# A two-layer hybrid mixer step on one core: TensorE's order fixed by a tracing weaver, with projections kept in DRAM

## The chip, the core and the metric

The kernel runs on one core of a Trainium2 chip as one launch. The metric is the device time of an execution in microseconds; the median of three runs of the kernel before is 1660.7 us (1656.93 to 1663.94). The profile is of a single execution, with its own time.

## The reference

One inference step of a bidirectional diffusion backbone with two layers, in float32, over 1280 tokens (256 of a prompt, which scan themselves from zero states, and 1024 latent tokens, which scan from cached states), model width 1024. Cut to what matters, per layer:

```
mod = silu(c) @ w_ada + b_ada                       # shift, scale, gate; for prompt and latent
h   = rmsnorm(x, g) * (1 + scale) + shift
proj = h @ w_in                                     # aq ak av ao az ag | bq bk bv bz | cq ck cv cz clr
A (4 heads x 128): stabilised chunkwise mLSTM, gates ag; times sigmoid(ao)
B (4 heads x 64):  retention, 2-D rotary on latent queries and keys
C (4 heads x 32/64): gated linear attention, decay from clr @ gla_w2
each: one scan forward + one backward, summed; y = head_rms(.) * headnorm_g * silu(az|bz|cz)
x   = x + gate * (y @ w_out)
```

At the end come a final RMS norm and the context's last states of both layers as outputs.

## The kernel before

The 1280 tokens are ten chunks of 128. The normalised input `h` stays in SBUF in two parts (a rounded high part and the rest), and every projection is three matmuls per 128 rows of `w_in` (`TERMS`, L467), accumulated in one of two PSUM banks `pj`. There are two forms. `mm_fm` (L469) has features on the partitions, in token blocks of 256, 512 and 512: 24 matmuls per block, 72 for 128 features; it serves queries, keys and the gates of `gate_z` (L1229). `mm_tm` (L488) has tokens on the partitions, 256 features for a pair of chunks: 48 matmuls per pair, 240 for all ten chunks; it serves values (`proj_v`, L516), output gates (`proj_o`, L1111) and `out_proj` (L1330). `gates` (L554) projects 304 columns per chunk (C's values and the small gate inputs). Weights come through two `raw` buffers and are split by ScalarE and VectorE (L433).

The mixers work in float32, in small steps that go through TensorE, ScalarE, VectorE and GpSimd in turn, in six PSUM banks `mx`. `mlstm_rows` (L580) makes the mLSTM's rows of weights and writes them to DRAM, `decays` (L660) C's cumulated decays. `group_c` (L743), `group_b` (L1017) and `head_a` (L1121, once for each of four heads) have the same two phases: a *key phase* over ten chunks (transpose the keys, scale them, multiply by the values, update the states) and an *output phase* over five pairs of chunks (scores, masking by decay weights, products, head norm, transposes, store). Their inputs and states live in twelve tiles of an arena `f5` (L128), which `proj_feat` (L508), `proj_v` and `proj_o` take as well. Every result goes to a DRAM tile `yd`, except the heads a2 and a3, whose results stay in the arena. `gate_z` reads it, multiplies by the gated projection and writes it back; `out_proj` loads all of it into the place of `h`.

The order of a layer is a hand-written string, which `layer` (L1247) goes through step by step:

```
"g v0 cq ck m d k1 C q0 k0 o0 a0 q1 z7 bg a1 z6 br bt bk0 bg bk1 bq0 bg bg bg bq1 be bv z1 B bg bg k2 "
"v1 bg bg q2 bg z0 bg bg k3 o1 bg a2 q3 a3 bg z5 z2 bg z4 z3 bg bg bg",          # layer 0
```

(`m` is `mlstm_rows`, `d` is `decays`, `bg` a piece of the background work that computes modulations on VectorE, 16 units in layer 0.) The string sets only the order of tracing and so of buffers. The order of each engine's instructions comes from the framework's scheduler, which lists instructions by simulated readiness and priority. Projections' matmuls are traced at a very low priority (`late`, L165), score matmuls at a high one and chained (`run`, L152), so that the scheduler puts projections wherever mixers leave room. DMAs are issued by SyncE, in the order of its queue.

## Time and profile before

| | |
|---|---|
| median of three runs | 1660.7 us |
| profiled execution, its own time | 1658.01 us |
| its span | 1656.2 us |
| mean granted TensorE clock | 0.980 |
| TensorE busy (matmul) | 1562.5 us, 94% |
| VectorE / ScalarE / GpSimd busy | 983.5 / 607.8 / 128.4 us |
| instructions | 28729 |
| DMA moved | 167.51 MB, mean 101 GB/s |

The span runs from the first to the last instruction. A matmul counts as busy from its issue to its modelled end, so neighbouring matmuls overlap, and the pace of a dense run is read from starts, not from the mean duration. The granted clock is 1.00 at 2.4 GHz; a mean of 0.98 over a stage says that TensorE ran part of it at 1.2 GHz. A float32 matmul of a mixer has two records, a transpose one.

### The profile page before, as it was taken

Reading aid. Unit: us, or ns where it says so; the run is one execution under the profiler, and the core shown is the slowest. Engines: PE = TensorE matmul, PEld = TensorE weight load, DVE = VectorE, ACT = ScalarE, POOL = GpSimd, SP = SyncE. Lnnn points to the kernel's source line nnn. Section 1 sums busy time; section 2 is a strip of 40 time slices with the busy share of each in tenths; the row PEclk is TensorE's granted clock in tenths of the full one; section 3 lists DMA queues with packets and bytes.
Section 4 is the critical chain, followed back from the end, with each engine's and each line's share of the span. In section 5 each row is a group of like instructions: output and inputs, shape, how many; then the busy total and the mean of one; then the engine's idle time right before and its main releaser. Section 6 shows DMA issues by size and latency. Waiting matters only on the chain.

```text
span 1656.2 us, 28729 instructions
## 1 busy us (share of the span) xinstructions
PE 1562.5 (94%) x11014; PEld 1423.2 (86%) x11014; DVE 983.5 (59%) x2510; ACT 607.8 (37%) x1587; POOL 128.4 (8%) x215
## 2 busy tenths in 40 slices
PE   6899889999999998999999889899999999999997
PEld 2898779887889897889999878899888989988997
DVE  3477765486778855863454676556336643465545
ACT  5546324333112324342365362244411223434323
POOL 1200010000001001000021000100000100000001
PEclk9999999999999999999999998999999999999999
DMA  9213143433424534561141031424233142336203
GB/s 326 71 41 83 49 115 92 140 118 104 123 62 129 163 101 118 191 183 38 36 161 39 18 87 29 122 77 115 59 88 100 34 136 80 111 109 189 64 14 130
DMA packets 169344, 167.51 MB, mean 101 GB/s; under 512 B 19101, under 2 KB 144957, under 8 KB 169197
## 3 DMA queue, kind: packets, MB, share of 16 engines
q1 hardware_dynamic: 169024, 165.53, 33.4%
q8 instruction: 88, 1.44, 0.4%
q14 instruction: 60, 0.48, 0.1%
q10 hardware_dynamic: 172, 0.05, 0.0%
HBM read 129.49 MB, written 27.85 MB: 95 GB/s over the span
## 4 chain that ended last, share of the span: by engine, by line
PE 66%; DMA 13%; DVE 12%; ACT 4%; issue 2%; SPq 1%; POOL 0%; DVEq 0%; POOLq 0%; ACTq 0%
PE pj L477 25%; PE pj L496 23%; DMA f<-in_w_ada_dram 3%; PE pj L567 3%; DMA rw<-rrow 3%; DMA f<-f 3%; PE mx L1203 2%; PE mx L1152 2%; DVE f L333 2%; DMA wk<-yd 2%; PE mx L1205 2%; PE mx L1194 1%; DVE f L535 1%; DVE lo L439 1%; PE mx L417 1%
## 5 line engine op out<-in xcount | busy, mean ns | idle before, releaser
L477 PE MATMUL pj<-hA,hi 128*128 128x512 f32 (+1 forms) x1408 | 373.3, 347 | 2.3 <-ACT f L504 2.3
L496 PE MATMUL pj<-hi,hA 128*128 128x256 f32 x1728 | 343.6, 286 | 5.7 <-ACT f L1118 2.2
L496 PEld LDWEIGHTS pj<-hi,hA 128*128 128x128 f32 x1728 | 276.3, 190 | 9.5 <-ACT f L1118 2.8
L477 PEld LDWEIGHTS pj<-hA,hi 128*128 128x128 f32 x1408 | 243.4, 191 | 31.1 <-ACT f L504 2.7
L496 PE MATMUL pj<-hi,hB 128*128 128x256 f32 x1152 | 240.4, 287 | 10.3 <-ACT f L504 6.3
L477 PE MATMUL pj<-hB,hi 128*128 128x512 f32 x704 | 237.2, 406 | 4.9 <-ACT f L504 2.5
L496 PE MATMUL pj<-lo,hA 128*128 128x256 f32 x864 | 241.0, 285 | 0.0
L477 PE MATMUL pj<-hA,lo 128*128 128x256 f32 (+1 forms) x704 | 240.7, 346 | 0.0
L496 PEld LDWEIGHTS pj<-hi,hB 128*128 128x128 f32 x1152 | 188.8, 190 | 12.7 <-ACT f L504 7.1
L439 DVE TENSOR_TENSOR lo<-raw,hi 128x256 fp32r<-128x256 f32 (+2 forms) x193 | 118.4, 625 | 114.3 <-ACT hi L438 107.6
L496 PEld LDWEIGHTS pj<-lo,hA 128*128 128x128 f32 x864 | 161.5, 189 | 0.3 <-issue 0.2
L496 PE MATMUL pj<-lo,hB 128*128 128x256 f32 x576 | 161.6, 285 | 0.0
L477 PEld LDWEIGHTS pj<-hB,hi 128*128 128x128 f32 x704 | 132.4, 192 | 33.7 <-ACT f L504 3.2
L438 ACT CAST hi<-raw 128x256 fp32r<-128x256 f32 (+2 forms) x193 | 106.5, 564 | 133.8 <-PE pj L477 98.0
L477 PEld LDWEIGHTS pj<-hA,lo 128*128 128x128 f32 x704 | 134.3, 191 | 14.8 <-issue 0.5
L477 PE MATMUL pj<-hB,lo 128*128 128x512 f32 x352 | 142.2, 404 | 0.0
L333 DVE SCALAR_TENSOR_TENSOR f<-f,sc 128x256 f32<-128x256 f32 x224 | 97.2, 479 | 23.2 <-DMA f<-in_w_ada_dram 23.1
L496 PEld LDWEIGHTS pj<-lo,hB 128*128 128x128 f32 x576 | 108.2, 190 | 0.0
L374 ACT ACTIVATE rw<-f 128x256 bf16<-128x256 f32 (+1 forms) x90 | 43.3, 482 | 112.3 <-DVE f L1374 106.3
L504 ACT COPY f<-pj 128x256 f32<-128x256 f32 (+2 forms) x142 | 48.5, 390 | 87.7 <-PE pj L496 48.0
L477 PEld LDWEIGHTS pj<-hB,lo 128*128 128x128 f32 x352 | 67.4, 192 | 14.7
L1371 DVE TENSOR_TENSOR wk<-pj,f 128x512 f32<-128x512 f32 (+1 forms) x45 | 28.3, 630 | 83.3 <-PE pj L496 82.6
(276 smaller groups left out, 2486.8 us busy)
## 6 DMA issues: line engine op xcount, KB each, us to landing
raw<-in_w_in_dram SPq DMA_DIRECT2D x64, 512.0 KB
f<-in_w_ada_dram SPq DMA_DIRECT2D x32, 384.0 KB
wk<-yd SPq DMA_DIRECT2D x48, 256.0 KB
rw<-rrow SPq DMA_DIRECT2D x40, 256.0 KB
rw<-wrow SPq DMA_DIRECT2D x40, 256.0 KB
f<-in_w_ada_dram SPq DMA_DIRECT2D x16, 512.0 KB
f<-in_x_sample_dram SPq DMA_DIRECT2D x16, 512.0 KB
raw<-in_w_out_dram SPq DMA_DIRECT2D x32, 256.0 KB
```

The source lines that it names most:

```text
L333: dve.scalar_tensor_tensor(acc[v], w, scv[:, k, v:v + 1], acc[v], ALU.mult, ALU.add)
L374: act.activation(rw().bitcast(BF16)[:, 0:x.shape[1]], x, AF.Square, accum_out=out)
L438: act.copy(hi[:, e], raw[:, e])
L439: dve.tensor_tensor(lo[:, e], raw[:, e], hi[:, e].bitcast(F32), ALU.subtract)
L477: pe.matmul(ps[:, :n], lhsT=w[wi][:, k, :], rhs=hblk(xi, k, b), start=(i == 0), stop=(i == 23))
L496: end = pe.matmul(pv[:, u, :], lhsT=hchunk(xi, k, c), rhs=w[e // 4][wi][:, e % 4, :], start=(i == 0), stop=(i == 23))
L504: act.copy(out, ps)
L567: pe.matmul(ps, lhsT=hchunk(xi, k, c), rhs=w[k // 3][wi][:, k % 3, :], start=(i == 0), stop=(i == 23))
L1152: pe.matmul(U[d], lhsT=ks[:, d * P:(d + 1) * P], rhs=v[:, c, :], start=True, stop=True)
L1203: pe.matmul(po[:, d, :], lhsT=r4[:, d, e, :], rhs=v[:, c, :], start=True, stop=not inter)
L1205: pe.matmul(po[:, d, :], lhsT=wb[:, d, e * P:(e + 1) * P], rhs=S[d][:, c, :], start=False, stop=True)
L1371: dve.tensor_tensor(t, pv, row.unsqueeze(1).to_broadcast([P, len(cs), 256]), ALU.mult)
```

## The change

Tracing is turned into cooperative threads. Each mixer, the chain of projections of the layers, the modulations, the norms and the gate multiplications become Python generators, which yield `wait(gap, cond, tiles needed)`. A weaver holds a clock that counts the traced matmuls' estimated cost, always continues the first thread (mixers before projections) whose gap has passed, whose condition holds and whose tiles are free, and chains every TensorE instruction to the one before it. So TensorE's order is the order of tracing. The other engines' instructions are still placed by the scheduler, but those of a mixer's visit not ahead of the last TensorE instruction traced before the visit.

```diff
+        def visit(self, th):
...
+            for ins in nc.cur_bb.bb.instructions[n:]:
+                if ins.engine == mybir.EngineType.PE:
+                    if self.tail is not None:
+                        edge(ins, self.tail, mybir.DependencyReason.DATA)
+                    self.tail = ins
+                    clock[0] += cost(ins)
+                elif th.mixer and tail is not None:
+                    edge(ins, tail, mybir.DependencyReason.SCHED_ONLY)
+            th.ready = clock[0] + gap
+
+        def run(self):
+            while self.threads:
+                best, kept = None, 0
+                for th in self.threads:
+                    n = th.need.get(f5, 0)
+                    t = None if n and len(f5.free) < kept + n else th.time()
+                    kept += n if th.cond is None or th.cond() else 0
+                    if t is not None and (best is None or t < best[0]):
+                        best = t, th
+                        if t <= clock[0]:
+                            break
...
+                clock[0] = max(clock[0], best[0])
+                self.visit(best[1])
```

`mm_fm` and `mm_tm` yield after pieces of 6 matmuls of 512 columns or 12 of 256; `late`, `run`, `not_before` and their priorities go. Both layers have one order, in which a `+` says that the projection's result is stored to DRAM slots `sp` and fetched by its mixer:

```diff
-    "g cq v0 ck m q0 d C k0 k1 o0 z6 br a0 q1 a1 bv bq0 bk1 z7 bt bk0 bq1 be z1 v1 q2 B z0 k2 k3 o1 a2 q3 "
-    "a3 z5 z2 z4 z3",
+    "g cq+ ck+ C k0+ v0+ q0+ o0+ a0 k1+ q1+ a1 bk0+ bk1+ bq0+ bq1+ bv+ B v1+ k2+ q2+ k3+ q3+ o1+ a2 a3 z",
```

```diff
+    def put(out, x, f):
+        if out[0].tensor.name == sp.tensor.name:
+            stage = wk()
+            f([v3(stage[:, x * i:x * i + x], o.shape[-1]) if len(o.shape) == 3 else stage[:, x * i:x * i + x]
+               for i, o in enumerate(out)])
+            for i, o in enumerate(out):
+                act.dma_start(o, v3(stage[:, x * i:x * i + x], o.shape[-1]) if len(o.shape) == 3
+                              else stage[:, x * i:x * i + x])
+        else:
+            f(out)
...
+    def fetched(x):
+        t, name = x
...
+            t = f5()
+            sync.dma_start(t, src)
```

A mixer's gaps stand in its generator. `decays` comes first, then `mlstm_rows` (gaps 9, 7, 8, 6, 2.5, 6) and `group_c` beside each other. The start and the loops of `group_c` and `head_a`, and the demand of `group_b`:

```diff
+    def group_c(l, e, finished):
...
+        yield wait(0, cond=lambda: "B" in e and "ck" in e, f=4, rw=1)
...
         for p in range(2):
+            yield wait(6.0, rw=1)
...
+        yield wait(7.0, mx=2, sm=2, sta=2)
...
+        for i in range(NCH + 1):
...
+            yield wait(2.5, mx=1, sm=1, sta=int(i < 2))
...
+        yield wait(0, cond=lambda: not inside, mx=4, rw=2)
+        inside.append(1)
+        tiles, yn = scores(0), None
+        for c0 in range(0, NCH + 2, 2):
+            yield wait(5.0, mx=2, rw=1, wk=1, ti=1)
...
+                yield wait(2.0, mx=4, rw=2)
+                tiles = scores(c0 + 2)
+        inside.clear()
...
+    def head_a(l, hd, e, finished):
+
+        yield wait(0, cond=lambda: "rows" in e, f=4, sta=2)
...
+        yield wait(6.0, mx=2, sm=2)
...
+            yield wait(2.2, mx=1, sm=1)
...
+        yield wait(0, cond=lambda: not inside, f=1, rw=4, sm=2)
...
+        yield wait(4.0)
+        weights(0, ahead[0])
+        yield wait(3.0, mx=1, rw=2, sm=1)
...
+        for c0 in range(0, NCH + 2, 2):
+            yield wait(5.0, mx=3, wk=1, ti=3)
...
+    def group_b(l, e, finished, general):
+        yield wait(0, f=9, sta=3, sm=1)
```

`group_b` then has four gaps of 7 (one per rotated tile), one of 8, ten of 2.5 in its keys, and 5.0 and 2.0 per output round. A mixer that is over lets `fillers` run its `gate_z`, behind the layer's projections in rank; `out_proj` waits until all of `gate_z` and, in layer 0, the modulations are done. The modulations become one thread of 16 units. Further edits: every head's result goes through `yd`, those of a2 and a3 too (`gate_z` and `out_proj` read them there); weight loads and their splits are traced with a priority 400 instructions ahead; the head norm of B and C works on two chunks at once; C's keys are scaled in three blocks; keys of the next chunk are transposed ahead of the products of the last; `mlstm_rows` needs three arena tiles instead of five; `rw` has 7 buffers instead of 8, `sm` 5 instead of 4, `ti` 8 instead of 4.

## Rows read from the trace of the kernel before

**Rows 1.** part 1 of the page: busy us, share of the span, instructions

```profile
PE 1562.5 (94%) x11014; PEld 1423.2 (86%) x11014; DVE 983.5 (59%) x2510; ACT 607.8 (37%) x1587; POOL 128.4 (8%) x215
```

**Rows 2.** busy time by stage: width, each engine (x instructions), PEclk, DMA share, GB/s

```profile
81.50:742.70 661.20, 626.60 (x4301) 564.65 (x4299) 462.78 (x1223) 232.59 (x601) 49.30 (x76) 0.98 0.39 113
...
898.00:1532.00 634.00, 609.50 (x4187) 552.30 (x4188) 352.74 (x920) 223.56 (x580) 44.91 (x66) 0.98 0.32 91
...
1532.00:1656.20 124.20, 111.25 (x910) 109.79 (x908) 64.18 (x167) 38.85 (x119) 5.43 (x10) 0.96 0.20 69
```

**Rows 3.** the same view of finer stages

```profile
180.00:260.00 80.00, 70.90 (x607) 64.36 (x608) 54.03 (x142) 21.97 (x57) 11.38 (x13) 0.96 0.29 80
...
898.00:990.00 92.00, 82.85 (x506) 72.99 (x506) 62.28 (x106) 43.97 (x66) 2.76 (x4) 0.96 0.25 64
...
990.00:1060.00 70.00, 61.41 (x480) 54.22 (x481) 46.05 (x112) 19.55 (x48) 7.21 (x7) 0.88 0.22 61
...
1060.00:1240.00 180.00, 178.27 (x1240) 164.58 (x1239) 87.34 (x254) 67.77 (x211) 13.69 (x26) 1.00 0.32 89
```

**Rows 4.** who waited for whom, TensorE: total us, times, longest us

```profile
PE mx L654 <- DVE sm L652: 8.8, 6, 2.2
PE pj L496 <- ACT f L504: 7.6, 7, 4.8
...
PE mx L811 <- DVE f L771: 3.7, 2, 3.2
```

**Rows 5.** TensorE's timeline at the layers' borders: start us, us, line, tiles, count

```profile
86.69 0.30 PE L567 MATMUL pj<-lo,hB 128*128 128x304 f32 x1
...
734.35 0.39 PE L477 MATMUL pj<-hB,lo 128*128 128x512 f32 x1
...
897.63 0.30 PE L567 MATMUL pj<-lo,hB 128*128 128x304 f32 x1
...
992.07 0.87 PE L811 MATMUL mx<-cst,f 128*128 128x128 f32 x6 [3.19 <-DVE f L771]
...
1525.42 0.39 PE L477 MATMUL pj<-hB,lo 128*128 128x512 f32 x1
```

**Rows 6.** the chain that ended last, two dense runs of projections: start us, us

```profile
1189.02 52.94 PE pj L477 x274
...
1535.54 82.53 PE pj L496 x676
```

**Rows 7.** TensorE's timeline, four float32 matmuls of a mixer

```profile
1301.51 0.66 PE L1028 MATMUL mx<-f,sm 128*128 128x128 f32 x4
...
1301.93 0.36 PE L496 MATMUL pj<-hi,hA 128*128 128x256 f32 x1
```

**Rows 8.** VectorE's timeline, first and last full-width operation of L580's rows

```profile
902.67 0.82 DVE L587 COPY f<-f 36x1280 f32<-36x1280 f32 x1
...
931.95 1.47 DVE L624 TENSOR_TENSOR f<-f,ti 36x1280 f32<-36x1280 f32 x1
```

**Rows 9.** ScalarE: one group by line (busy, mean ns, idle before); one DMA issue

```profile
L504 ACT COPY f<-pj 128x256 f32<-128x256 f32 (+2 forms) x142 | 48.5, 390 | 87.7 <-PE pj L496 48.0 <-PE pj L477 19.7 <-PE pj L567 15.5
...
1.17 0.47 ACTq L195 DMA_DIRECT2D wk<-in_headnorm_g_dram  x1
```

**Rows 10.** DMA queue (packets, MB, share); SyncE's longest waits (total, times, longest)

```profile
q1 hardware_dynamic: 169024, 165.53, 33.4%
...
SPq L445 <- DVE lo L439: 168.1, 28, 32.4
```

**Rows 11.** the chain at the end of layer 1: start us, us

```profile
1508.19 2.05 DMA yd<-wk
1510.25 3.21 DMA wk<-yd
```

More of the change, by code (lines that the diff above doesn't have):

```diff
@@ L100, in __init__, with take, give @@
         def __init__(self, name, n, cols, space=sb, dt=F32):
[L101 to L102 removed]
+            self.free = [space.tile([P, cols], dt, tag=f"{name}{i}", name=f"{name}{i}") for i in range(n)]
+            self.n, self.at = n, {}
         def __call__(self):
[L105 to L106 removed]
+            t = self.take()
+            self.give(t)
+            return t
+        def take(self):
+            return self.free.pop(0)
+        def give(self, *tiles):
+            for t in tiles:
+                self.free.append(t)
+                self.at[id(t)] = clock[0] + HELD
     class Arena:
@@ new lines, in wait, with cost @@
+    def wait(gap=0.0, cond=None, **need):
+        return gap, cond, {pools[k]: n for k, n in need.items()}
+    def cost(ins):
+        out, lhs = ins.outs[0].bass_ap, ins.ins[0].bass_ap
+        n = 1
+        for a in out.shape[1:]:
+            n *= a
+        if out.shape[0] < 2 or lhs.shape[0] < 64 and n > 64:
+            return 0.06
+        if ins.is_transpose:
+            return 0.11
+        if lhs.dtype == F32R:
+            return 0.007 + 0.441 * n / 1000
+        return 2 * max(0.109, 0.84 * n / 1000) * (0.5 if lhs.shape[0] < P else 1)
@@ L430, in norm_h, with norm_thread @@
             f5.give(*xn)
+    def norm_thread(l, b, xn, done):
+        yield wait(5.0, mx=1, rw=1)
+        for k in range(KT):
+            norm_h(l, b, xn, [k])
+            if k < KT - 1:
+                yield wait(0.9, mx=1, rw=1)
+        done.add(b)
     def split(raw, parts=1, cols=1024):
@@ L603, in mlstm_rows @@
         dve.tensor_tensor(r, F, m, ALU.subtract)
-        mp, rl_, al = (ti()[0:R, 0:NCH] for _ in range(3))
+        yield wait(8.0)
+        small = [ti.take() for _ in range(3)]
+        mp, rl_, al = (t[0:R, 0:NCH] for t in small)
         mc = v3(m, P)
@@ new lines, in group_b @@
+        fin = ring[2]
+        last = None
+        yield wait(8.0, mx=2, sm=2)
+        for i in range(len(order) + 1):
+            if i < len(order):
+                bank = mx.take()
+                now = bank, keys(1, order[i], bank[:, 0:256])
+            if i > 0:
+                c, (bank, ks) = order[i - 1], last
+                U = products(ks, c, bank[:, 256:512])
+                if c == 0:
+                    update(fin, sbv(0), U, 1)
+                    state_out(fin, 1)
+                else:
+                    update(sbv(c - 1), sbv(c) if c != 1 else None, U, 1)
+                mx.give(bank)
+            last = now
+            yield wait(2.5, mx=1, sm=1)
@@ L1430, in program, with modulations, layers @@
                 late_setup()
-        for l in range(2):
-            out_proj(l, layer(l, general, w))
+        anchor[0] = None if general else adas[-1].ins
+        normed, prepared = set(), set()
+        def modulations():
+            yield wait(40.0)
+            yield from background()
+            prepared.add(0)
+        def layers():
+            yield wait()
+            yield from layer(0, general, w, lambda c: True, lambda: general or prepared)
+            yield from out_proj(0, normed)
+            yield from layer(1, general, w, lambda c: (c + 2) // 4 in normed, lambda: True)
+            yield from out_proj(1, normed)
+        weave.add(layers(), 2)
+        if not general:
+            weave.add(modulations(), 1)
+        weave.run()
         pn = mx()
```

1070 lines of the change are left out of this document (630 added, 440 removed), and 2 rows, old and new, of the table ORDER.

## The prediction

> **What bounds the kernel now.** I read the busy shares first: TensorE is busy 94% of a span of 1656.2 us [rows 1], so only its order, its waits and its clock can move the time. By stage, the two stretches of projections and mixers hold 661 and 634 us, with 34.6 and 24.5 us in which TensorE has nothing, while VectorE is at 70% and 56% [rows 2]. These holes lie close together. Finer stages show 9.1 us in 180 to 260 and 9.2 and 8.6 us in 898 to 990 and 990 to 1060, where the granted clock falls to 0.96 and 0.88; the 180 us behind, with two heads in work, lose 1.7 us at a clock of 1.00 [rows 3]. So mixers woven densely into projections can be nearly free, and the holes are stages without enough projections to put between them. TensorE's waits agree: behind the start none is longer than 5 us, and they are on small mixer steps and on evacuations into arena tiles [rows 4]. An evacuation there waits until one of twelve tiles is free.
>
> The layers' borders give the two lengths that the change acts on [rows 5]: from the last gate matmul to the last matmul of `gate_z`, 87.0 to 734.7 in layer 0 (647.7 us) and 897.9 to 1525.8 in layer 1 (627.9 us). Start, output projections and end (380 us together) keep their order and tiles; I take them over.
>
> **Work in a layer.** 274 projection matmuls over features took 52.94 us and 676 over tokens 82.53 us [rows 6]: 0.193 and 0.122 each. `proj_feat` and `gate_z` run 22 times with 72 matmuls (13.9 us each, 306 us); the five token projections 240 each (29.3 us, 147 us). Layer 1's stage holds 4187 matmuls; without these 2784 and some 50 of the next stage, 1350 are the mixers'. Four of theirs took 0.42 us [rows 7], so at most 142 us, and less where row tiles run side by side; I estimate 110 to 142. TensorE's work is thus 563 to 595 us per layer, 33 to 85 us under what the layers take now. Spilled tiles make projections independent of the arena, so they can fill every hole while they last. That is the gain.
>
> **The mixers' chain.** The new order has a length of its own. One mixer at a time may be in its output phase (`inside`), group B needs nine of the twelve arena tiles, and each visit comes a traced gap after the one before. A gap ends at a piece's border; pieces are 6 matmuls of 512 or 12 of 256 columns, 1.4 us, so a gap costs 0.7 more on average. Own matmuls of a visit are priced at 0.21 (two records). Counted from the end of the gates:
> - C waits for cq and ck (28 + 2.5), then gaps 6, 6, 7 (21), 11 key visits of 2.5 + 0.7 + 0.7 (43) and five output rounds of 12 with a last visit (64): 158.
> - a0 and a1, keys done meanwhile: prelude 9, six gaps of 5.7, matmuls 12, so 55 each: 268.
> - B is traced behind ten feature and three token projections (227) and the mixers' matmuls so far (50): 277. Four rotations of 7.7 and 8.7 (39), ten key visits of 3.9 (39), outputs 80: 435.
> - a2 cannot load before B returns its tiles: 48 for loads and keys, 55 for outputs: 538. a3 outputs 51, with less to put between: 589. The last `gate_z` piece set, 14: **603**.
> This is more than the work, so the chain sets the layer's length: for its last part the projections have run out and TensorE waits for a2 and a3. The half pieces weigh most: some 95 gaps are on the chain, so without them it is 536, under the work; with whole pieces 670.
>
> **New waits.** TensorE's order is fixed, so a visit that comes too early holds every projection piece behind it, and the evacuations behind those.
> - Start of a layer. C's first key transposes stand about 51 us behind the gates (30 + 21). Now they start 94 us behind them (992.1 against 897.9) [rows 5], after the mLSTM rows, the decays and C's preparation. The rows' stretch on VectorE took 31 us (902.7 to 933.4) [rows 8]; they no longer have to come first, but share VectorE. 94 - 31 = 63, 12 late; I take 14. Bounds: 0, as VectorE was idle for 30 of these 92 us [rows 3], and 43, if nothing overlaps.
> - Layer 0 also carries the sixteen modulation units; its VectorE is busier by 110 us [rows 2]. I add 5; bounds 0 and 20.
> - Output visits. Not priced above 0; bounds 0 and 20 per layer, one late microsecond for each of some twenty visits in the filled part; in the dense stage of two heads TensorE lost 1.7 us in 180 [rows 3], the nearest row, hence 0.
> - Stores. Each layer evacuates 42 feature blocks through `wk` with one DMA from ScalarE and 25 token pairs with two: 92 issues of 0.47 [rows 9], 43 us of ScalarE, which is busy 233 of 661 us [rows 2]. An evacuation of 0.39 [rows 9] plus one or two issues is under the 2.8 us of the shortest block, with two banks: 0. Bounds 0 and 43, all uncovered.
> - Loads. SyncE gets some 60 more DMAs per layer; it stood up to 32.4 us before a weight load whose buffer was in use [rows 10], and a fetch behind such a wait is late by what is left of it. Fetches are traced a phase ahead: 0, bounds 0 and 32 once a layer.
> - End of a layer. y2 and y3 now go through DRAM; a store and a load took 2.05 and 3.21 [rows 11]. `out_proj` takes these blocks last: 2, bounds 0 and 5.3.
> - Merged head norms, C's keys scaled in three blocks and one row tile fewer change VectorE and GpSimd by a few us each way, beside work that already covers them: 0.
>
> **One rule weighed.** The queue moved 165.5 MB in 33.4% of the engines' span [rows 10]. Spilled slots add 24 x 0.66 MB of stores and some 19 MB of loads per layer, about 70 MB: by the row, 48%.
> The Trainium skill (DMA: Bandwidth & Descriptors, "Issuing engines are not separate DMA queues") says that DMAs from ScalarE and SyncE share the same 16 engines, so the second queue buys issue time only. By that rule the stores slow the loads: if landing times grew with the share, the layer's end would cost 3 where I took 2. No run here shows both queues loaded.
>
> **The sum.** Layer 0: 603 + 14 + 5 + 2 = 624 instead of 647.7, -23.7. Layer 1: 603 + 14 + 2 = 619 instead of 627.9, -8.9. Together -32.6: a span of 1623.6. The profiled execution took 1658.0 with its span of 1656.2, so 1625.4; the median of the three runs is 2.7 above it. On that scale: **1628 us**, 2% faster.
>
> **Rivals.**
> - *The work sets the end* (0.16). If gaps cost little more than their traced length, the chain is under the work and projections last to the end: layers of about 580, -67.7 and -47.9, so 1656 - 116 + 4.5 = 1545. For it: the dense 180 us [rows 3]. Against it: a2 and a3 both stand behind B.
> - *Waits move, none go* (0.12). What a hole cost is paid at the fixed visits: 1661, at most some us either way. For it: most holes are at layer starts, where VectorE's chain of rows, decays and preparation is the same.
> - *VectorE is late for the fixed order* (0.30). At the start of a layer C's keys are 28 late instead of 14, and some twenty output visits 1 us each: 603 + 28 + 20 + 2 = 653, in layer 0 658. That is +10.3 and +25.1, so 1696. Stalls of 32 us per layer decide: 603 + 32 + 2 is the present mean of 638. For it: TensorE has no other instruction to take while it stands, and VectorE, at 68% in 898 to 990 [rows 3], is what C's first keys wait for already, up to 3.2 us [rows 4]. Against it: its idle 30 us in that stretch.
> - That values stay in the arena after all is excluded: every name in the new order has the sign for the spill, and every mixer fetches.
>
> **How the numbers follow.** The forecast case has 0.42 and reaches from 1605 to 1650: layers 12 shorter to 11 longer than in the sum. About 0.5% (8 us) is what a measurement of this kernel can tell from no change. Faster: 0.42 + 0.16 = 0.58; same 0.12; slower 0.30. For 8 in 10 the range takes in most of the first rival and of the slow one, and the half pieces' bounds: 1555 to 1700.
>
> **What would show it.** TensorE's idle time in 180 to 260 and 990 to 1060 should fall under 3 us per stage, at a clock near 1.00. A wait of 10 us or more at C's first transposes in each layer would show the start's price, named as a wait for VectorE; none would take 28 us off. Sparse TensorE between the last `gate_z` of B and that of a3, with granted clock at 1.2 GHz there in part, would show the chain; a dense end there would prove the first rival. More than ten output visits that wait a microsecond or more for VectorE would prove the slow one, and a wait of an evacuation for a store would show that the stores are not hidden. The prediction is wrong if either layer, gates' end to last `gate_z`, takes under 590 or over 650 us.

## The result and the profile after

The changed kernel takes 1787.5 us (median of 4 runs, 1782.6 to 1789.5) against 1662.3 in the same comparison (1656.9 to 1665.2): ratio 1.0753, 95% interval 1.0715 to 1.0791. It is 125 us slower. The forecast was 1628, and the result lies above its range, which ended at 1700. The profiled execution took 1789.2 with a span of 1787.4, at a mean granted clock of 0.950 (0.980 before).

Part 1 of the page after, and the busy time by stage, cut at the gates' end and the last `gate_z` of each layer (width, engines, granted clock, DMA share, GB/s):

```profile
PE 1598.8 (89%) x11014; PEld 1457.6 (82%) x11014; DVE 987.6 (55%) x2458; ACT 607.5 (34%) x1555; POOL 113.0 (6%) x193
```
```profile
89.50:781.80 692.30, 619.84 (x4197) 561.12 (x4196) 450.63 (x1174) 216.89 (x554) 42.30 (x66) 0.96 0.49 151
781.80:975.80 194.00, 173.76 (x1296) 168.13 (x1294) 80.81 (x159) 80.48 (x212) 11.55 (x20) 0.93 0.27 84
975.80:1637.70 661.90, 609.30 (x4138) 552.21 (x4137) 345.80 (x880) 214.07 (x550) 40.78 (x62) 0.97 0.44 134
1637.70:1787.40 149.70, 127.17 (x963) 122.88 (x961) 75.56 (x185) 47.63 (x137) 5.44 (x10) 0.90 0.30 93
```

These answer to [rows 1, 2]. TensorE's matmuls fill 89% of the span instead of 94%, while VectorE and ScalarE have within 5 us the work that they had, and GpSimd 15 us less: TensorE stood more. It was also slower where it worked: the same 11014 matmuls fill 36 us more (1598.8 against 1562.5). In the traces TensorE is busy at the lower level of the clock, 1.2 GHz, for 121 us here and for 53 before. Half of that difference, 34 us, is an estimate of what the clock alone cost. The other 95 of the 131 us by which the spans differ are time without a matmul. By the borders of [rows 5], layer 0 takes 692 us instead of 647.7, layer 1 662 instead of 627.9, the stretch between them 194 instead of 163.3, the stretch behind layer 1 150 instead of 130.8: 44 + 34 + 31 + 19 = 128 of those 131. So two things went wrong, inside the layers and at their ends, and the forecast had the second at 2 us a layer.

What TensorE waited for (total us, times, longest us), in answer to [rows 4], and the timeline of C's second key transposes in each layer, in answer to the line of L811 in [rows 5] (the first had stood alone since 146.68 and 1029.57):

```profile
PE mx L1554 <- DVE rw L1576: 28.2, 9, 6.6
PE mx L998 <- DVE f L953: 25.2, 2, 12.9
PE mx L1554 <- DVE rw L1507: 21.4, 20, 2.7
PE pj L579 <- ACT hA L1686: 19.2, 13, 5.5
PE mx L1247 <- DVE sm L1249: 13.3, 8, 3.1
PE mx L1254 <- DVE sta L1266: 10.8, 8, 1.7
PE pj L579 <- ACT wk L588: 9.7, 2, 7.3
...
PE mx L429 <- DVE f L419: 3.3, 1, 3.3
```
```profile
159.23 0.45 PE L998 MATMUL mx<-cst,f 128*128 128x128 f32 x1 [12.28 <-DVE f L953]
...
1042.75 0.47 PE L998 MATMUL mx<-cst,f 128*128 128x128 f32 x1 [12.90 <-DVE f L953]
```

Before, the largest of these groups was 8.8 us. Now there are five of over 10 us inside the mixers (L1554 twice, L998, L1247, L1254; 99 us together) and one at `out_proj` (L579 waiting for the casts of y, 19.2). C's keys stand for 12.3 and 12.9 us, close to the 14 that the forecast gave them. The 20 waits at L1554 for L1507 are one pattern inside the visits of `head_a`. One of these visits, with the other engines' rows between:

```profile
333.11 0.61 PE L1506 MATMUL mx<-f,f 128*128 128x128 f32 x4
...
333.84 0.68 DVE L1507 TENSOR_TENSOR rw<-rw,mx 128x512 f32<-128x512 f32 x1
...
334.57 0.44 PE L1554 MATMUL mx<-cst,rw 128*128 128x128 f32 x2 [0.85 <-DVE rw L1507]
```

The four score matmuls (L1506) go to one half of a PSUM bank, VectorE multiplies them into a tile (L1507, from 333.84 for 0.68), and the transposes of the round before (L1554), which read no result of that multiplication, go to the bank's other half. They start at 334.57, 0.05 after VectorE is done. In a fixed order nothing else may go in between.

The Trainium skill (PSUM — Partial Sum Buffer, "PSUM bank collisions raise a hardware error") gives the rule to guard accesses to PSUM with semaphores by bank and quadrant of partitions, or simply by bank, not by address. The trace agrees with a guard by bank: the transposes touch no address that VectorE reads, and yet they wait until the read's end.

In the kernel before, none of these groups shares a bank with work that does not depend on it. There the scores have a bank of their own, the transposes go into the bank of their own round's products, and B's keys take one bank per chunk. So the change did two things here: it put these groups into halves of one bank, which the description above does not list, and it fixed their order.

### The profile page after: what moved, and what is told of

It is laid out like the page before. It is cut to its first block, busy times and chain, and to the rows that moved or that the text cites. A ratio compares the mean times of both kernels' runs of the same rounds, so it can differ in the third digit from the quotient of the medians.

```text
span 1787.4 us, 29167 instructions
## 1 busy us (share of the span) xinstructions
PE 1598.8 (89%) x11014; PEld 1457.6 (82%) x11014; DVE 987.6 (55%) x2458; ACT 607.5 (34%) x1555; POOL 113.0 (6%) x193
## 5 line engine op out<-in xcount | busy, mean ns | idle before, releaser
L566 PE MATMUL pj<-hA,hi 128*128 128x256 f32 (+1 forms) x1408 | 366.0, 351 | 7.6 <-DVE wk L1597 7.6
L579 PE MATMUL pj<-hi,hA 128*128 128x256 f32 x1728 | 340.6, 297 | 24.4 <-ACT hA L1686 19.2
L579 PEld LDWEIGHTS pj<-hi,hA 128*128 128x128 f32 x1728 | 285.5, 202 | 33.4 <-ACT hA L1686 23.4
L566 PEld LDWEIGHTS pj<-hA,hi 128*128 128x128 f32 x1408 | 243.4, 196 | 34.3 <-DVE wk L1597 8.4
L579 PE MATMUL pj<-lo,hA 128*128 128x256 f32 x864 | 252.2, 292 | 0.0
L566 PE MATMUL pj<-hA,lo 128*128 128x512 f32 (+1 forms) x704 | 241.8, 343 | 0.0
L579 PE MATMUL pj<-hi,hB 128*128 128x256 f32 x1152 | 215.8, 288 | 9.7 <-ACT wk L588 9.7
L566 PE MATMUL pj<-hB,hi 128*128 128x512 f32 x704 | 223.8, 399 | 0.0
L579 PEld LDWEIGHTS pj<-hi,hB 128*128 128x128 f32 x1152 | 182.4, 195 | 10.6 <-ACT wk L588 10.1
L579 PEld LDWEIGHTS pj<-lo,hA 128*128 128x128 f32 x864 | 173.9, 201 | 0.0
L579 PE MATMUL pj<-lo,hB 128*128 128x256 f32 x576 | 164.6, 286 | 0.0
L566 PEld LDWEIGHTS pj<-hA,lo 128*128 128x128 f32 x704 | 137.2, 195 | 15.5
L566 PEld LDWEIGHTS pj<-hB,hi 128*128 128x128 f32 x704 | 128.6, 189 | 24.9
L566 PE MATMUL pj<-hB,lo 128*128 128x512 f32 x352 | 138.2, 393 | 0.0
L579 PEld LDWEIGHTS pj<-lo,hB 128*128 128x128 f32 x576 | 112.1, 195 | 0.0
L419 DVE SCALAR_TENSOR_TENSOR f<-f,sc 128x256 f32<-128x256 f32 x224 | 96.2, 479 | 16.3 <-DMA f<-in_w_ada_dram 16.1
L588 ACT COPY wk<-pj 128x256 f32<-128x256 f32 (+1 forms) x102 | 40.8, 431 | 115.7 <-PE pj L566 67.6
L566 PEld LDWEIGHTS pj<-hB,lo 128*128 128x128 f32 x352 | 66.3, 188 | 14.5
```

Source lines behind the costliest of these rows:

```text
L419: dve.scalar_tensor_tensor(acc[v], w, scv[:, k, v:v + 1], acc[v], ALU.mult, ALU.add)
L566: pe.matmul(ps[:, :n], lhsT=w[wi][:, k, :], rhs=hblk(xi, k, b), start=(i == 0), stop=(i == 23))
L579: pe.matmul(pv[:, u, :], lhsT=hchunk(xi, k, c), rhs=w[e // 4][wi][:, e % 4, :], start=(i == 0), stop=(i == 23))
L588: act.copy(out, ps)
```

## The experiments

All ratios are to the kernel before in the same comparison, so 1.0753 is the mark of the changed kernel; 0.01 is 16.6 us.

### Is it the traffic of the spilled tiles?

`e3_double_stores`: each store is issued twice, the second into slots that nothing reads.

```diff
-            for i, o in enumerate(out):
+            for i, o in list(enumerate(out)) + list(enumerate(twin)):
                 act.dma_start(o, ...
```

> Every store of a spilled block is issued twice, the second into a second set of slots in DRAM that nothing reads: 184 more issues on ScalarE and some 31 MB more traffic. Theory traffic: what the stores and their issues cost is paid a second time; if they make up most of the 125 us between the two kernels, at least 40 more, 1827 or above. Theory order: the issues lie on an engine that is busy 607 of 1787 us, so within 10 of 1787.

1795.5 us, ratio 1.0781 [1.0744, 1.0818]: 0.0028 more, some 5 us, within both intervals. The queues (packets, MB, share) of the changed kernel and of this one:

```profile
q1 hardware_dynamic: 199040, 206.18, 37.7%
q10 hardware_dynamic: 26668, 31.52, 5.0%
```
```profile
q1 hardware_dynamic: 199040, 206.18, 37.9%
q10 hardware_dynamic: 53164, 62.99, 10.0%
```

The second queue moved twice as much, and the time that the first one's packets took stayed at 38%. So the stores are not the cause. The fetches were not doubled; that they are not the cause either follows from `e10_free_y_ahead` below, which has them all and is as fast as the kernel before. The rule weighed in the forecast (the Trainium skill, DMA: Bandwidth & Descriptors, "Issuing engines are not separate DMA queues"), that DMAs from all issuing engines run on the same 16 engines and interleave, would let stores slow the loads. In this run the first queue's share rose by 0.2 points. (The changed kernel's two queues take 42.7% together; the forecast had 48%.)

### Does a stall that is taken away come back?

`e2_key_gap` puts projections where TensorE stood before C's first keys:

```diff
-        yield wait(7.0, mx=2, sm=2, sta=2)
+        yield wait(20.0, mx=2, sm=2, sta=2)
```

> The traced gap ahead of C's first key transposes is 20 instead of 7, so that projections stand there where TensorE waited 12.9 and 12.3 us in the two layers. If the work of TensorE sets a layer's length, the waits there go and the time falls by about 25, to 1762. If the chain of mixers sets it, the projections used up here are missing at the layer's end, where TensorE then stands longer: the waits at C's keys go, those at head_a's output transposes grow by the same amount, and the time stays within 6 of 1787. Theory traffic: no change of the time either, but no growth at the end.

1790.5 us, 1.0744 [1.0709, 1.0779]: nothing gained, though the wait at L998 is gone. The wait at the modulations' transposes (L429, in layer 0 alone) grew from 3.3 to 12.0 us, and those at `head_a`'s transposes behind VectorE's last multiplication (L1576) from 28.2 to 31.8:

```profile
PE mx L1554 <- DVE rw L1576: 31.8, 10, 8.1
...
PE mx L429 <- DVE f L419: 12.0, 1, 12.0
```

The time is as the chain of mixers would have it, the waits are not: those at `head_a`'s output transposes were to grow by the 25 us that went, and grew by 3.6. By the borders of its trace the two layers differ: layer 1 is 9.6 us shorter (1640.66 - 988.25 = 652.4 instead of 662.0), layer 0 is 10.2 longer. So in layer 1, in this one execution, most of the stall did come back as time.

`e4_b_first` shortens the chain: B directly behind C, so that the heads need no second start, and projections last to the end.

```diff
-    "g cq+ ck+ C k0+ v0+ q0+ o0+ a0 k1+ q1+ a1 bk0+ bk1+ bq0+ bq1+ bv+ B v1+ k2+ q2+ k3+ q3+ o1+ a2 a3 z",
+    "g cq+ ck+ C bk0+ bk1+ bq0+ bq1+ bv+ B k0+ v0+ q0+ o0+ a0 k1+ q1+ a1 v1+ k2+ q2+ a2 o1+ k3+ q3+ a3 z",
...
-        yield wait(0, cond=lambda: not inside, f=1, rw=4, sm=2)
+        yield wait(0, cond=lambda: not inside and f"q{hd}" in e and f"y{hd}" in e, f=1, rw=4, sm=2)
```

(and layer 0 ends once 12 of the 16 modulation units are done, the other four being layer 1's.)

> B is traced behind C, ahead of the four heads, with its projections right behind C's; a head's output phase waits until its q and output gate are projected; the four modulation units that only layer 1's out_proj reads no longer hold up the end of layer 0. The mixers' work and the projections are the same. Theory order: the heads then follow one another with no second start behind B, projections last to the layer's end, the waits at head_a's output transposes in the last 60 us of each layer (17.7 us in 640-840 of the changed kernel) go, and each layer is 25 to 45 shorter: 1700 to 1740. Theory traffic: as many stores and loads, closer together: within 15 of 1787.

1786.6 us, 1.0722 [1.0680, 1.0764]: a miss for the chain. The sparse end is gone, as expected (the waits behind L1580, which is L1576 in the changed kernel, fell from 28.2 us to 2.1), and the time is the same: TensorE waited 12.4 us for heads' keys from DRAM (L1445) and 10.4 at L429 in their place. `e7_b_first_gap` takes C's stall out of this kernel with the edit of `e2_key_gap`, `e8_b_first_all` takes several out at once. Both have a second edit that their expectations do not name, and so have the later runs with B first: the heads a2 and a3 load only when a0 and a1 are over.

```diff
-        yield wait(0, cond=lambda: "rows" in e, f=4, sta=2)
+        yield wait(0, cond=lambda: "rows" in e and (hd < 2 or f"d{hd - 2}" in e), f=4, sta=2)
```

> The kernel with B ahead of the heads (1786.6 us), with the gap ahead of C's first key transposes at 20 instead of 7. In the changed kernel the same edit gave nothing (1790.5). If that was because the chain of mixers set the layer's length there, and it doesn't with B first, where projections last to the end, the 24 us that TensorE waits there in the two layers now come back: 1760 to 1768. If a stall that is taken away always turns up at a later visit, the time stays within 6 of 1787.

1788.0 us, 1.0745 [1.0724, 1.0766]: no gain again, from the two edits together. Waits turned up elsewhere, at evacuations (L570, waiting for ScalarE's L592 and L594 to empty a bank) and at the heads' transposes behind L1580 (2.1 us in the kernel with B first, 13.2 now):

```profile
PE mx L1558 <- DVE rw L1580: 13.2, 5, 4.1
...
PE pj L570 <- ACT wk L594: 9.5, 2, 5.7
...
PE pj L570 <- ACT wk L592: 6.7, 2, 5.1
```

> The kernel with B ahead of the heads, with all the single remedies at once: the gap of 20 ahead of C's keys, five y blocks read ahead into arena tiles (which gave 17.7 alone), a gap of 10 instead of 2 ahead of the modulations' transposes (10.4 us waited there), 9 instead of 6 ahead of a head's first keys (12.4 us waited there for its tiles from DRAM), and shorter gaps inside a modulation unit. If the stalls add up: 1787 - 24 - 18 - 20 = 1725, 1715 to 1740. If taking one away makes another: above 1755. Neither theory has it under the kernel before.

1786.6 us, 1.0738 [1.0718, 1.0759]: nothing, on the side of "another appears". So neither the stores, nor a single gap, nor B's place in the order holds these kernels at 1787.

### Is it the fixed order?

`e5_free_order` leaves out the edges by which the weaver ties the order, and nothing else; the scheduler then places each engine's instructions as it did before.

```diff
     def edge(ins, end, reason):
-        tc.add_manual_dep(ins, end.name, mybir.DependencyInfo(mybir.DependencyClass.NoSync, reason), reason="weave")
+        pass
```

> The edges that tie every TensorE instruction to the one traced before it, and the mixers' other work to it, are left out; the visits, their gaps, tiles and spills stay. The builder's scheduler then orders each engine as it thinks best. Theory fixed order (TensorE stands because one order, with gaps shorter than the other engines' real latencies, lets nothing pass): the waits at C's first keys (25 us), at head_a's output transposes (50) and at B's keys and products (24) fall by half or more, and the time to 1690-1750. Theory layout (the arena's twelve tiles, one output phase at a time, projections in the traced sequence and the spilled tiles set the chain, whatever the order on TensorE): the time stays within 15 of 1787.

1708.4 us, 1.0278 [1.0258, 1.0298]: 79 us back, more than any other edit gave. The waits, the layers' borders and one output visit of this kernel:

```profile
PE pj L579 <- ACT hA L1686: 25.1, 9, 11.3
...
PE mx L1554 <- DVE rw L1507: 5.2, 2, 4.9
```
```profile
96.83 0.30 PE L698 MATMUL pj<-lo,hB 128*128 128x304 f32 x1
...
738.62 0.39 PE L566 MATMUL pj<-hB,lo 128*128 128x512 f32 x1
...
930.84 0.30 PE L698 MATMUL pj<-lo,hB 128*128 128x304 f32 x1
...
1547.82 0.40 PE L566 MATMUL pj<-hB,lo 128*128 128x512 f32 x1
```
```profile
333.03 0.39 PE L1506 MATMUL mx<-f,f 128*128 128x128 f32 x2
...
334.18 0.47 PE L566 MATMUL pj<-hB,hi 128*128 128x512 f32 x1
...
337.49 0.28 PE L566 MATMUL pj<-hA,hi 128*128 128x256 f32 x1
337.61 0.38 PE L1554 MATMUL mx<-cst,rw 128*128 128x128 f32 x2
```

The waits at C's keys for VectorE (25.2 us) came down to 1.6, those at B's keys and products are gone, and those at L1554 for L1507 fell from 21.4 to 5.2. The visit shows how: between its last scores (L1506) and the transposes of the round before (L1554) the scheduler put 18 projection matmuls (L566, 334.18 to 337.49). Of the pairs of transposes found in the traces, 7 of 39 have no projection directly in front of them here, 32 of 38 in the changed kernel and 11 of 40 in the kernel before. Layer 0 takes 641.8 us and layer 1 617.0, both less than before. What is left over the kernel before lies at the ends: 192.2 from the last `gate_z` to the next gates' end (163.3 before), where L579 waits up to 11.3 us for y's casts.

`e6_free_late` gives the projections' matmuls the low priority of the kernel before as well:

```diff
+            with late():
                 for wi, xi in TERMS:
                     pe.matmul(ps[:, :n], ...
```

> As the run with the free order, and the projections' matmuls have the low priority that they had in the kernel before, so that a mixer's ready instruction goes first and projections fill what is left. Theory fixed order: at least as fast as with the free order alone, 1670-1740, as this undoes the main part of the change. Theory layout: within 15 of 1787, as the chain through arena, output phases and spilled tiles is the same.

1750.5 us, 1.0520 [1.0483, 1.0557]: better than the fixed order, but 42 us worse than the scheduler without it. That was a miss. `e9_pe_order_only` asks which of the two kinds of edges costs:

```diff
-                elif th.mixer and tail is not None:
-                    edge(ins, tail, mybir.DependencyReason.SCHED_ONLY)
```

> TensorE's order stays tied as in the changed kernel (1787.5); only the second kind of edge is left out, which keeps the mixers' work on the other engines behind the TensorE instruction traced before it. If TensorE's fixed order is what costs the 79 us that the free order gave back: 1770 to 1795, with the waits at first keys and output transposes as they were. If the ties of the other engines hold VectorE's work back and so make it late: 1700 to 1740.

1853.7 us, 1.1148 [1.1107, 1.1189]: slower by 66 us, which neither theory had. The ties of the other engines are a help to a fixed TensorE. Without them its transposes wait longest of all runs for VectorE:

```profile
PE mx L1552 <- DVE rw L1574: 57.8, 12, 16.6
PE mx L1552 <- DVE rw L1505: 34.3, 22, 4.9
```

### Which part of the fixed order?

`e13_visit_order` keeps the order tied and changes the sequence inside three visits: transposes ahead of scores in `head_a`, both key transposes ahead of their reading and both products ahead of their updates in B.

```diff
-            if ahead:
-                scores(c0 + 2, ahead[0], other[:, 0:256])
             if before is not None:
                 ...
                     pe.transpose(pt[:, u * P:(u + 1) * P], hp[:, u * P:(u + 1) * P], ident)
+            if ahead:
+                scores(c0 + 2, ahead[0], other[:, 0:256])
...
-            return [keys(0, a, bank[:, 256 * i:256 * i + 256]) for i, a in enumerate((c, c + 1)) if a < 9]
+            for a, pk in halves:
+                turned(a, pk)
+            return [keys(0, a, pk, False) for a, pk in halves]
```

> The changed kernel (1787.5) with TensorE's order still fixed; only inside three visits is the sequence another: in head_a's output visits the transposes of the round before stand ahead of the scores (20 waits of 1.1 us stood between scores and transposes, for VectorE's reading of the scores in the other half of the same bank), in B's visits both pairs of key transposes stand ahead of VectorE's reading (8 waits, 13.3 us), and both pairs of products ahead of the state updates (8 waits, 10.6 us). No gap, tile or load is changed. If back-to-back matmuls in a visit that wait on the bank's other half make up the fixed order's price: 45 us less, 1735 to 1750. If the chain of mixers with its real latencies sets the time, and TensorE's waits only show it: within 12 of 1787, with the waits at other lines.

1750.9 us, 1.0506 [1.0478, 1.0535]: 37 of the 45 us are real. The same visit now (L1560 are the transposes, L1514 the scores), and the list's head:

```profile
331.60 0.39 PE L1523 MATMUL mx<-f,rw 128*128 128x129 f32 x2
331.82 0.38 PE L1560 MATMUL mx<-cst,rw 128*128 128x128 f32 x2
332.04 0.61 PE L1514 MATMUL mx<-f,f 128*128 128x128 f32 x4
```
```profile
PE mx L1560 <- DVE rw L1584: 29.7, 9, 4.7
PE mx L998 <- DVE f L953: 25.1, 2, 12.9
PE pj L579 <- ACT hA L1694: 19.5, 14, 5.5
```

The transposes follow the products without a wait, and B's waits are gone from the trace; those for the round before (L1584, formerly L1576), C's keys and `out_proj`'s casts stayed.

### The end of a layer

`e12_before_y_dram` does this part alone to the kernel before: y2 and y3 through DRAM.

```diff
-            if hd < 2:
-                sync.dma_start(yd[hd], y)
-                f5.give(y)
+            sync.dma_start(yd[hd], y)
+            f5.give(y)
...
-                if k in (2, 3):
-                    yv = ys[k - 2][:, t0:t0 + n]
-                else:
-                    yv = wk()[:, :n]
-                    sync.dma_start(yv, yd[k, :, t0:t0 + n])
+                yv = wk()[:, :n]
+                sync.dma_start(yv, yd[k, :, t0:t0 + n])
```

> The kernel before (1661), with one part of the change alone: y2 and y3 go to DRAM behind their heads and come back for gate_z and out_proj through the three staging tiles, as the other six blocks do. The prediction priced this at 2 per layer: 1665 to 1672. If it is what makes the stretches behind the last gate_z 29 and 27 longer in the run with the free order: 1700 to 1720.

1721.0 us, 1.0326 [1.0284, 1.0368]: 54 us for an edit that the forecast had at 4. Borders and wait:

```profile
748.03 0.40 PE L477 MATMUL pj<-hB,lo 128*128 128x512 f32 x1
...
939.22 0.30 PE L567 MATMUL pj<-lo,hB 128*128 128x304 f32 x1
...
1575.94 0.40 PE L477 MATMUL pj<-hB,lo 128*128 128x512 f32 x1
```

```profile
PE pj L496 <- ACT hA L1336: 24.1, 12, 7.7
```

From layer 0's last `gate_z` to the next gates' end it is 191.2 us (163.3 before), from layer 1's to the span's end at 1726.7 it is 150.8 (130.8): 48 us at the ends. In the kernel before, L496 waited 1.5 us in all for the casts; here it is 24.1 for ScalarE's alone. (The profiled execution was the slowest of four: its span is 70.5 longer than before, and the other 22 us lie inside the layers. 34.5 of the 70.5 are longer matmul time, 1597.0 against 1562.5, at a clock of 0.960.)

The casts show what happens. Each layer has 24 casts (eight y blocks in three parts). In the kernel before, 13 of them stand ahead of the last `gate_z` matmul, and the last cast starts 15.4 and 17.4 us behind that matmul. Here none stands ahead of it, and the last starts 39.8 and 41.0 behind it; in the changed kernel it is none, 39.7 and 37.9. The last `gate_z`, that of y3, now needs the three staging tiles `wk` itself, where it had y in the arena before, so the reloads for the casts come behind it.

`e1_y_ahead` mends part of it in the changed kernel: y blocks are read into arena tiles while the last head works, 11 in the two layers by its trace.

```diff
+        def ahead():
+            while len(ys) < 6 and not closed:
+                yield wait(0, cond=lambda: closed or "a2" in over and len(ys) < len(gated)
+                           and clock[0] >= gated[len(ys)][1] and len(f5.free) - weave.reserved() >= 3)
+                if not closed:
+                    kt = gated[len(ys)][0]
+                    ys[kt] = f5()
+                    sync.dma_start(ys[kt], yd[kt])
```

> Five of the eight y blocks of each layer are read from DRAM into arena tiles while the last head is still at work, instead of behind its last gate_z; the rest is as in the changed kernel (1787.5 us). Theory order (the changed order leaves places where TensorE must stand, and the end of each layer is one): the waits of out_proj's matmuls for the casts of y, 16.8 and 16.4 us in the two layers of the changed kernel, fall to under 5 each, and the time by 20 to 30, to 1757-1767. Theory traffic (stores and loads of the spilled tiles slow the transfers everywhere): the loads are as many as before and as slow, only earlier, so the time falls by under 8.

1769.9 us, 1.0623 [1.0589, 1.0657]: 0.0130 or some 20 us, while the waits for the casts fell only in number (13 to 5, still 19 us). `e10_free_y_ahead` frees the order, reads y blocks ahead (up to seven, by its trace six a layer) and lets the last `gate_z` write its block straight into `out_proj`'s input:

```diff
+            if last:
+                cast(kt, b, yv)
+                ys[kt] = None
+            else:
+                sync.dma_start(yd[kt, :, t0:t0 + n], yv)
```

> Free order (1708.4), and the end of a layer mended: y blocks are read ahead into arena tiles as in the run that did so alone (-17.7), and the last gate_z writes its block straight into out_proj's input instead of to DRAM and back. With the free order the two layers, gates' end to last gate_z, took 641.8 and 617.1 against 647.7 and 627.9 before, and what is left over the kernel before is the stretch from the last gate_z to the next gates' end (192 against 163) and to the end (157 against 130). If y's way through DRAM and three staging tiles is its cause: 1708 - 45 = 1663, 1650 to 1678, no slower than the kernel before. If it is the tail of the mixers' chain instead: above 1690.

1663.3 us, 0.9996 [0.9978, 1.0013]: as expected to a microsecond, and no different from the kernel before. Casts stand ahead of the last `gate_z` matmul again, 21 and 16 of 24, and the last one starts 16.7 and 16.1 us behind it. The borders, the wait for casts, and the reads ahead (times issued; ns of an issue; first and last start):

```profile
100.60 0.30 PE L698 MATMUL pj<-lo,hB 128*128 128x304 f32 x1
...
740.11 0.39 PE L566 MATMUL pj<-hB,lo 128*128 128x512 f32 x1
...
909.85 0.30 PE L698 MATMUL pj<-lo,hB 128*128 128x304 f32 x1
...
1528.64 0.39 PE L566 MATMUL pj<-hB,lo 128*128 128x512 f32 x1
```
```profile
PE pj L579 <- ACT hA L1610: 6.9, 2, 5.2
```
```profile
L1650 SPq DMA_DIRECT2D f<-yd x12: 320/423/861, 669.9 to 1471.2; - x12
```

### What is left for a faster kernel

`e11_free_b_first` is the free order with B first (both its edits as above).

> Free order with B ahead of the heads and the four late modulation units, as in the run with B first (1786.6 with the fixed order). If with the free order the chain through B's nine tiles and a second start of heads behind it sets the layers: 20 to 40 under 1708, 1668 to 1690. If TensorE's work sets them: 1700 to 1715.

1696.3 us, 1.0194 [1.0165, 1.0223]: 14 us less than the free order alone by the ratios, a little short of the expected 20. `e14_free_best` puts the mended end, B first and the new visits on the free order:

> All that helped with the free order together: the free order with y read ahead (1663.3), B ahead of the heads (-12 with the free order), and the new sequence inside the visits. If these add up: 1640 to 1652, faster than both kernels by some 1%. If y's repair and B's place met the same stretch: 1658 to 1668, as the kernel before.

1695.7 us, 1.0193 [1.0164, 1.0222]: outside both forecasts. But the run did not contain what it was to test. Its trace has no read of y into an arena tile; `out_proj` fetched all blocks but the last through the staging tiles, 42 parts in two layers where `e10_free_y_ahead` has 6:

```profile
L1728 SPq DMA_DIRECT2D wk<-yd x42: 319/320/373, 752.4 to 1574.9; - x42
```

So what a mended end is worth with B first stays open. `e15_fixed_best` puts mended end, new visits and C's gap on the fixed order:

> The same repairs with the fixed order and the order of the change: y read ahead and the last gate_z direct, the new sequence inside the visits, and the gap of 20 ahead of C's keys. With the free order the first of these gave 45, in the fixed order a part of it 18. If stalls of the fixed order are local and add up: 1787 - 35 - 45 - 10 = 1697, 1685 to 1710. If the chain takes back all but the layer's end: 1745 to 1765.

1709.8 us, 1.0273 [1.0245, 1.0301]: 78 of 125 us back without touching the fixed order, 13 short of the sum. Against `e10_free_y_ahead`, which has the same mended end and a free order, 46 us are left (0.0277). `e16_start_tied` ties only the first 38 us of the traced clock on top of `e10_free_y_ahead`, `e17_best` adds the new visits.

```diff
+        if clock[0] < 38.0:
             tc.add_manual_dep(ins, end.name, ...
```

> The free order with the layer's end mended (1663.3), but TensorE tied to the traced order up to the end of layer 0's gates: with the free order these ended at 100.6, with the fixed one at 89.5, in the kernel before at 87.0. If that difference at the start is the order's and nothing behind gives it back: 1652, 1648 to 1656, faster than the kernel before by 0.5 to 0.9%. If the mixers' first steps set the time from there: 1660 to 1666.

1661.5 us, 0.9982 [0.9968, 0.9996]. Layer 0's gates still ended at 101.8, so the tie did not do what it was to do. With an interval just under 1 it is the best kernel here, 3 us ahead of the kernel before, less than the 0.5% that I would call a difference.

> The same with the new sequence inside head_a's and B's visits (which gave 36.6 with the fixed order). With the free order nearly none of those waits are left (5.2 us at the output transposes), so 0 to 8 less than the run without it: 1645 to 1655. If the new sequence costs where the scheduler chose another (with B first, the free order and this sequence together were no faster): above 1658.

1670.3 us, 1.0031 [1.0016, 1.0046]: 8 or 9 us worse, as the second forecast had it. The visits' new sequence helps where the order is fixed and costs a little where the scheduler has its own.

## Why the prediction was wrong

By ratios the 0.0753 come apart into 0.0475 that the fixed order costs (`e5_free_order`), 0.0282 for the layers' ends (`e10_free_y_ahead`) and -0.0004 for all the rest, spills, pieces, gaps and loads. That split is shown, in this sequence of undoing. The forecast was 160 us lower. It had 28 for the first (the starts of the two layers) where 79 stand, 4 for the second where 47 stand, and a gain of 65 for the rest, of which the sum shows nothing.

- **The failing step, "Output visits".** The forecast had them at 0, at most 20 us a layer, from a stage in which two heads ran densely. In that stage of the kernel before, 7 of 10 pairs of output transposes have a projection directly in front of them: the scheduler had filled the visits' insides, and [rows 3] showed its work, not the visit's nature. The order now fixed puts products, scores and transposes back to back, and B's pairs likewise, in halves of one bank. The waits inside the visits (L1554 for L1507, L1247, L1254) sum to 45.5 us, 23 a layer; new sequences alone gave 37 us of time back (`e13_visit_order`). The forecast counted one wait per visit, at its head, and none inside. A bank for each group under the fixed order was not tried. The other 42 of the 79 us are the fixed order's too, but no run shows where they arise.
- **The second failing step, "End of a layer".** Priced at 2, bounds 0 and 5.3, from one store and one load. In its place stand 28 and 20 us (`e12_before_y_dram`); mending it gave 45 to 47 (`e10_free_y_ahead`). A transfer's length was the wrong measure. A block can be cast only behind the last projection that reads the input it overwrites, and its reload needs a staging tile; behind the last `gate_z` all reloads queue for three of them. How much of it is the tiles and how much the last block's own round trip was not separated. `e14_free_best`, where in effect only the last block's way is mended, hints at a smaller part for the latter: its two ends are 6.5 and 5.1 us shorter than in `e11_free_b_first`, while `e10_free_y_ahead` has them 22.5 and 21.5 shorter than `e5_free_order`.
- **The clock has no term.** Every wait was priced as the time for which TensorE stands. Of the 131 us between the spans 36 are longer matmul time, nearly all of it by the estimate above from the lower clock (0.950 instead of 0.980 on the mean).
- **The chain of 603.** It was to set the layer's length. With the 14 of the start, the sum has C's output end 172 us behind the gates, B start at 291 and end at 449, and the last `gate_z` end at 617. In layers 0 and 1 of the changed kernel these stand at 181 and 176, 328 and 317, 509 and 490, 692 and 662. So the head was right, and most of the delay came between C and B and inside B. "Keys done meanwhile" was wrong: a0 is traced behind q0 and o0, and its keys began at 259 and 1142, shortly before C ended (271 and 1152). Also, the 536 "without half pieces" was too low by the sum's own working: B starts at 277 behind its projections, whatever the 40 or so gaps of C, a0 and a1 cost, so only some 55 gaps lie behind that and the figure is 565. The sign named for the chain, a sparse end at a fallen clock, was there (12.0 us of matmuls in 740 to 766, last fence below), and the nine waits at L1554 for L1576 (28.2 us) all stand in a2 and a3. But taking that end away (`e4_b_first`) changed nothing, so this chain alone was not what held the time.
- **Start of a layer.** As a wait it was right: 12.3 and 12.9 where 14 stood. As a price it held in layer 1 at most; in layer 0 other waits took its place (`e2_key_gap`).
- **Stores and loads at 0** were nearly right (`e3_double_stores` for the stores). TensorE's list of waits has none for a fetch, and 6.8 us in all for the splits of weights (5.8 before). Of its two waits for an evacuation into a staging tile (L588, 9.7 us), the 7.3 us came at 437, while ScalarE prepared B's tables; the other 2.5 us came at 1312, behind a store on ScalarE's queue that by the profile stood until a fetch had landed.
- **The gain from spilled projections** exists but is small: with order and ends mended the layers take 639.5 and 618.8 us by the borders above (740.11 - 100.60 and 1528.64 - 909.85), 8 and 9 less than before, where 24 and 9 were forecast. A later start (gates' end at 100.6 instead of 86.7) takes 14 of the 17 back, and the two ends, still 6 and 4 longer than before, the rest.
- **"Start, output projections and end keep their order and tiles"** left 380 us out of the sum; 50 of the 131 us between the spans were there.
- **The slow rival** (1696, chance 0.30) had the right side and the right sentence, that TensorE has nothing else to take while it stands. Its sign came: 28 waits of a microsecond or more at L1554, L1247 and L1254. Its sizes were wrong: 12.6 instead of 28 at the start, its twenty visits of one microsecond were found (21.4 us), but ten in each layer, and B's visits and the layers' ends were not in it.

What stays open: why the stalls that were taken out of the fixed order one by one, at C's keys and in `e8_b_first_all`, gave no time back in the sum, when those inside the visits did. The traces show where other waits grew, not why there.

## What to carry to other kernels

An order that is fixed ahead must know every wait inside a step, not only the gap between steps: two matmul groups that share a bank with a reader between them belong apart, or in the other sequence. Before a block's way is changed from SBUF to DRAM, look at what its reload queues behind where the stage ends, not at the transfer. And undo the change's parts one at a time, and look in the trace whether the part was really undone: leaving out the ties, which removes no work at all, had the largest effect, and a read ahead that never took place looked like one that gave nothing.

## What the runs showed of the hardware

Two halves of one PSUM bank were not used side by side: in the visit shown, a matmul into one half started 0.05 us after VectorE's read of the other half ended, and 20 such waits took 21.4 us. The wait is that of a semaphore in this program; what the chip would do without it no run shows. And where TensorE had stood, the granted clock was lower. Stretches of the changed kernel, columns as above: C's keys in layer 0, the sparse end of layer 0, and the start of its `out_proj`:

```profile
137.00:160.00 23.00, 10.72 (x88) 10.52 (x87) 22.72 (x47) 6.20 (x12) 1.17 (x1) 0.76 0.36 98
740.00:766.00 26.00, 12.00 (x69) 11.19 (x70) 21.73 (x79) 8.13 (x34) 4.63 (x9) 0.75 0.67 227
782.00:800.00 18.00, 9.25 (x32) 6.52 (x31) 6.39 (x14) 5.00 (x13) 0.21 (x1) 0.64 0.63 184
```

At 0.64 to 0.76 on the mean, TensorE ran part of each stretch at 1.2 GHz, with about half of it filled by matmuls. Over the whole execution the mean clock was 0.950 in the changed kernel, 0.962 with the free order, 0.977 with the ends mended and 0.980 before, and the time of the 11014 matmuls 1598.8, 1579.9, 1557.6 and 1562.5 us. Counted at the higher level (the busy time at 1.2 GHz halved, an estimate from the traces) it is 1538, 1537, 1532 and 1536 us: the same work each time.
